# First feed-forward of a two-block transformer kernel: gate and up products as 2x2 blocks in seven instead of eight

## The chip, the cores and the metric

The kernel runs on one NeuronCore of a Trainium2 chip. The metric is the device time of one launch in microseconds (us), the median of several runs. Five engines work in parallel, and each carries out its own instructions strictly in order: TensorE (PE in the rows; PEld is its weight load), VectorE (DVE), ScalarE (ACT), GpSimd (POOL) and SyncE (SP), which here issues the DMA transfers.

## The reference, cut to what matters

Two blocks follow each other on x (512 tokens, width 1024). The first has two layers with a context of 256 tokens beside x; the second has feed-forwards, attention, a recurrence and a convolution. What is changed is the feed-forward of the first layer, which runs over x and context together, 768 tokens:

```
def swiglu(h, wg, wu, wd):
    return (jax.nn.silu(h @ wg) * (h @ wu)) @ wd
...
x = x + g_f * swiglu(rmsnorm(x) * (1 + sc_f) + sh_f, w_gate[l], w_up[l], w_down[l])
if ctx_out:
    ctx = ctx + mc[5] * swiglu(rmsnorm(ctx) * (1 + mc[4]) + mc[3], w_gate[l], w_up[l], w_down[l])
```

wg and wu are 1024 x 2816, wd is 2816 x 1024. The modulation vectors of layer 1 (`mod = silu_c @ w_ada[l] + b_ada[l]`, for x and for the context) don't depend on x, and the kernel computes most of them while this feed-forward runs.

## The kernel before, in words

All activations are kept transposed: features on the 128 partitions, the 768 tokens as columns (256 of the context, then 512 of x). A matmul in full fp32 precision is made of three matmuls in a rounded format: each operand is split into a rounded high part and the low rest (h and lo of a weight, ah and al of an activation), and `mm3` issues h*ah (L245), h*al (L246) and lo*ah (L247) for each of 8 blocks of 128 inner features. A weight tile comes by one DMA (`wtile`, L229), ScalarE copies it into the high part (L230), VectorE subtracts for the low part (L232). Activations are split likewise (`split`, L212 on ScalarE, L213 on VectorE).

`Ffn` computes a feed-forward. The 2816 inner rows are 22 blocks f of 128. For each f the weights of gate and up are loaded (512 KB each), both products are made over the 768 columns in two segments (256 and 512), `glu` takes silu of the gate on ScalarE (L409), multiplies with the up product on VectorE (L410) and splits the result. The inner rows come in groups, for the first feed-forward `G3 = ((0, 8), (8, 15), (15, 22))`; after each group the down product of its rows is made for 8 output blocks n, and VectorE adds it to x (`evac`, L1138). The last `tn` output blocks are done segment by segment so that the next phase can begin.

Ahead of the first feed-forward (phase `f0`) stands the first mixing phase, whose last part (`outproj`, then the norm with its modulation, L531 and L535) makes the activations of the feed-forward chunk by chunk; the first gate and up products are woven into it (`mm3k`, L260 to L262). Layer 1's modulation columns are made by `mod_cols`: one DMA of 512 KB (L493) a column, then for x and for the context each a product with a sum over 1024 elements, either in one VectorE instruction (L498) or as a product on GpSimd (L500) and a summing pass on ScalarE (L501). `MODV` says which. `_weave` mixes this stream with the feed-forward by declared costs (`MCOST`).

Memory is handed out by two allocators, `arena` (fp32) and `rarena` (rounded operands). A further piece, `room`, belongs to one of them at a time; `share` closes it and reopens it for the other, and everything that used it must have ended by then. The order in which each engine runs its instructions is set at build time by a scheduler that simulates a timeline; on the chip each engine then runs its list in order.

## Time and profile before

| | |
|---|---|
| median of 3 runs | 3878.45 us (3872.4 to 3878.79) |
| the profiled execution: its time, its span | 3877.54 us, 3875.8 us |
| TensorE busy | 3704.2 us, 96% of the span, mean granted clock 0.976 |
| VectorE busy | 1975.8 us, 51% |
| ScalarE busy | 1345.3 us, 35% |
| GpSimd busy | 591.6 us, 15% |
| first feed-forward, steady part | about 613 to 1100 us of the span |

The time is that of the whole launch; the span runs from the first to the last instruction. Busy shares are means over all stages, so for a change in one stage the rows of that stage are read. Times of instructions include their fill: matmuls overlap, and the distance from one start to the next is what a matmul costs.

### The profile page before, as it was taken

The page shows a single profiled execution, that of the slowest core. Times are in us where ns is not written, and L with a number is a line of the kernel's source. Part 1 is how long each engine was busy: PE and PEld are TensorE (multiplying, and loading weights), DVE is VectorE, ACT ScalarE, POOL GpSimd, SP SyncE. Part 2 cuts the span into 40 slices and gives each one's busy share as a digit, 9 for nine tenths or more (in the row PEclk, how much of TensorE's full clock was granted, in tenths as well). Part 3 has the DMA queues.
Part 4 walks back from the last instruction along what each step waited for, and adds up shares of the span by engine and source line. Part 5 has one row for each costly group of instructions (what it writes and reads, how often), then busy time and mean ns, then how long its engine had stood idle before and what let it go on. Part 6 is the DMA issues. An engine that isn't in the chain of part 4 may idle for free. (4 is left out here: it accounts for less than half of the span.)

```text
span 3875.8 us, 50567 instructions
## 1 busy us (share of the span) xinstructions
PE 3704.2 (96%) x20474; PEld 3203.6 (83%) x20474; DVE 1975.8 (51%) x3638; ACT 1345.3 (35%) x2263; POOL 591.6 (15%) x539
## 2 busy tenths in 40 slices
PE   6998899999999988999999998999999999999998
PEld 5776788888887778888988896798888888888887
DVE  8687756443254666333542358653236333736233
ACT  4233544431232354322332335443223222324222
POOL 3331012540013421000100021020002000211001
PEclk8998999999998999999999999999999999999999
DMA  5222115452202112322122321123222222312222
GB/s 208 66 93 67 39 40 181 144 181 92 61 33 74 39 65 71 103 94 91 66 95 92 110 75 51 55 90 102 81 98 98 98 75 95 109 66 98 98 94 75
DMA packets 95834, 345.12 MB, mean 89 GB/s; under 512 B 10864, under 2 KB 14064, under 8 KB 95600
## 3 DMA queue, kind: packets, MB, share of 16 engines
q1 hardware_dynamic: 95024, 341.37, 26.6%
q8 instruction: 160, 2.62, 0.3%
q14 instruction: 74, 0.61, 0.0%
q10 hardware_dynamic: 576, 0.52, 0.0%
HBM read 334.51 MB, written 4.19 MB: 87 GB/s over the span
## 5 line engine op out<-in xcount | busy, mean ns | idle before, releaser
L245 PE MATMUL psum<-rarena,room 128*128 128x512 f32 (+1 forms) x3121 | 1092.9, 351 | 5.1 <-ACT rarena L212 2.6
L247 PE MATMUL psum<-rarena,room 128*128 128x512 f32 (+1 forms) x3053 | 1076.4, 353 | 0.8 <-DVE room L232 0.8
L246 PE MATMUL psum<-rarena,room 128*128 128x512 f32 (+1 forms) x3065 | 1074.9, 351 | 0.5 <-DVE rarena L213 0.5
L247 PE MATMUL psum<-rarena 128*128 128x512 f32 (+1 forms) x2108 | 744.7, 354 | 9.9 <-DVE rarena L232 9.5
L245 PE MATMUL psum<-rarena 128*128 128x512 f32 (+1 forms) x2040 | 735.1, 361 | 16.2 <-ACT rarena L212 5.8
L246 PE MATMUL psum<-rarena 128*128 128x512 f32 (+1 forms) x2008 | 720.0, 359 | 1.3 <-DVE rarena L213 1.3
L245 PEld LDWEIGHTS psum<-rarena,room 128*128 128x128 f32 x3121 | 592.8, 190 | 82.5 <-ACT rarena L212 3.0
L246 PEld LDWEIGHTS psum<-rarena,room 128*128 128x128 f32 x3065 | 582.4, 190 | 76.0 <-DVE rarena L213 0.8
L247 PEld LDWEIGHTS psum<-rarena,room 128*128 128x128 f32 x3053 | 580.0, 190 | 78.7 <-DVE room L232 1.0
L232 DVE TENSOR_TENSOR room<-arena,room 128x1024 fp32r<-128x1024 f32 (+2 forms) x250 | 325.3, 1306 | 531.9 <-PE psum L246 231.5
L230 ACT ACTIVATE room<-arena 128x1024 fp32r<-128x1024 f32 (+2 forms) x290 | 320.1, 1110 | 738.0 <-DMA arena<-gu 242.1
L299 POOL TENSOR_TENSOR arena<-arena 128x256 f32<-128x256 f32 x170 | 136.5, 810 | 2282.8 <-ACT arena L297 2212.9
L247 PEld LDWEIGHTS psum<-rarena 128*128 128x128 f32 x2108 | 403.1, 191 | 64.2 <-DVE rarena L232 10.4
L245 PEld LDWEIGHTS psum<-rarena 128*128 128x128 f32 x2040 | 391.6, 192 | 75.5 <-ACT rarena L230 6.9
L246 PEld LDWEIGHTS psum<-rarena 128*128 128x128 f32 x2008 | 385.7, 192 | 54.6 <-DVE rarena L213 1.7
L230 ACT ACTIVATE rarena<-arena 128x1024 fp32r<-128x1024 f32 (+2 forms) x138 | 154.7, 1122 | 334.3 <-DMA arena<-gu 123.6
L232 DVE TENSOR_TENSOR rarena<-arena,rarena 128x1024 fp32r<-128x1024 f32 (+2 forms) x98 | 131.4, 1342 | 235.5 <-ACT rarena L230 114.9
L212 ACT ACTIVATE rarena<-arena 128x512 fp32r<-128x512 f32 (+2 forms) x257 | 131.2, 528 | 206.2 <-DVE arena L410 179.5
L213 DVE TENSOR_TENSOR rarena<-arena,rarena 128x512 fp32r<-128x512 f32 (+1 forms) x246 | 149.3, 622 | 87.9 <-ACT rarena L212 87.6
L297 ACT ACTIVATE arena<-arena 128x256 f32<-128x256 f32 (+1 forms) x274 | 106.9, 412 | 239.2 <-DVE arena L1230 117.3
L410 DVE TENSOR_TENSOR arena<-arena,psum 128x512 f32<-128x512 f32 (+1 forms) x170 | 100.5, 598 | 157.2 <-PE psum L247 150.9
L500 POOL TENSOR_TENSOR arena<-arena 128x1024 f32<-128x1024 f32 x48 | 125.4, 2619 | 199.9 <-DMA arena<-w_ada 88.9
(391 smaller groups left out, 4327.8 us busy)
## 6 DMA issues: line engine op xcount, KB each, us to landing
arena<-gu SPq DMA_DIRECT2D x264, 512.0 KB, 3.7
arena<-dn SPq DMA_DIRECT2D x80, 704.0 KB, 4.1
arena<-w_ada SPq DMA_DIRECT2D x60, 512.0 KB, 3.4
room<-w_ada SPq DMA_DIRECT2D x36, 512.0 KB, 4.0
room<-w_in SPq DMA_DIRECT2D x30, 512.0 KB, 3.3
arena<-c_in SPq DMA_DIRECT2D x24, 512.0 KB, 3.2
arena<-dn SPq DMA_DIRECT2D x16, 448.0 KB, 3.4
room<-ab_in SPq DMA_DIRECT2D x14, 512.0 KB, 3.2
```

What stands on the lines that cost most here:

```text
L212: A.activation(h, src, AF.Copy)
L213: eng.tensor_tensor(lo, src, h.bitcast(F32), ALU.subtract)
L230: A.activation(h.r, r.f, AF.Copy)
L232: (G if wlo[1] < wlo[0] else V).tensor_tensor(lo.r, r.f, h.f, ALU.subtract)
L245: PE.matmul(ps, h[:, s], ah, start=k == 0, stop=False)
L246: PE.matmul(ps, h[:, s], al_, start=False, stop=False)
L247: PE.matmul(ps, lo[:, s], ah, start=False, stop=k == nk - 1)
L297: A.activation(sq.f, src, AF.Square)
L299: (V if self.fast else G).tensor_tensor(self.parts[0].f, self.parts[0].f, sq.f, ALU.add)
L410: V.tensor_tensor(s.f, s.f, pu, ALU.mult)
L500: G.tensor_tensor(t.f, r.f, sic[q].f, ALU.mult)
```

## The change

The first feed-forward treats its inner blocks f = 2 to 21 as ten pairs. A pair of inner blocks (two block rows of output), the two halves of the 1024 features and the two halves of the 768 columns (384 each) form a 2x2 by 2x2 block product, which is computed with seven block products instead of eight (the form with 15 sums).

- `quads` loads the two weight tiles of gate (or up) of a pair raw, makes 4 sums of 128 x 512 and 7 splits (a copy on ScalarE, a subtract on VectorE) of 128 x 512; before, there were two splits of 128 x 1024.
- `seven_ops` and `combos` make the sums of the activation blocks once: 16 adds on GpSimd (`whole`, L555), 12 subtracts on VectorE (L562), 4 more (L390) and 12 splits, all 128 x 384. They run after the activations are complete. `third` puts the last sum in the place of one activation block once f = 1, the last plain one, is done (L580, L581).
- `Seven` makes each block product with matmuls of 384 columns (`prod`, L266 to L268) and adds the products up: per pair and per gate or up one ScalarE copy and five VectorE adds of 384 columns that read PSUM. `pair` takes silu, product and split on the four 384-column results (L603 and what follows).
- The groups of inner rows become six, `G3 = ((0, 4), (4, 8), (8, 12), (12, 16), (16, 18), (18, 22))`, so the evacuation of the down product runs six times rather than three, and its weight tiles are 128 x 512 (one group 128 x 256) rather than 1024 and 896.
- `room` is split into two parts; during the first feed-forward the first stays with `rarena` and the second goes to `arena`. The allocators' limits for temporaries are changed for that time (`BODY`), and freed extension space counts as last used when it is opened.
- All modulation products of layer 1 go to VectorE (`MODV`), so GpSimd loses 48 products and ScalarE 48 summing passes in this phase; the declared costs change (`MCOST`), and the first modulation columns are finished one by one (`each`). The number of output blocks done segment by segment at the end goes from 3 to 5 (`TN0`).

All else is the same code, but the whole program is scheduled anew.

```diff
-G3 = ((0, 8), (8, 15), (15, 22))
+G3 = ((0, 4), (4, 8), (8, 12), (12, 16), (16, 18), (18, 22))
...
-MLEN = 152 * UNIT
+ROOMS = (96 * UNIT, 56 * UNIT)
...
+        def prod(ps, w, acts, start, stop):
+
+            h, lo = w[0].r, w[1].r
+            for k, (ah, al_) in enumerate(acts):
+                s = slice(k * 128, k * 128 + 128)
+                f, e = start and k == 0, stop and k == len(acts) - 1
+                PE.matmul(ps, h[:, s], ah, start=f, stop=False, skip_group_check=True)
+                PE.matmul(ps, h[:, s], al_, start=False, stop=False, skip_group_check=True)
+                PE.matmul(ps, lo[:, s], ah, start=False, stop=e, skip_group_check=True)
...
+        def quads(src1, src2, n, eng):
+
+
+            r1, r2 = al(2 * n), al(2 * n)
+            SP.dma_start(r1.f, src1)
+            SP.dma_start(r2.f, src2)
+            a1, b1, a2, b2 = r1.f[:, :n], r1.f[:, n:], r2.f[:, :n], r2.f[:, n:]
+            yield split_new(a1, n, eng[0])
+            s2 = al(n)
+            eng[7].tensor_tensor(a1, a1, a2, ALU.subtract)
+            eng[8].tensor_tensor(s2.f, b2, a1, ALU.subtract)
+            yield split_new(s2.f, n, eng[1])
+            yield split_new(b1, n, eng[2])
+            eng[9].tensor_tensor(a2, a2, b2, ALU.add)
+            yield split_new(a2, n, eng[3])
+            yield split_new(a1, n, eng[4])
+            eng[10].tensor_tensor(s2.f, b1, s2.f, ALU.subtract)
+            yield split_new(s2.f, n, eng[5])
+            fr(s2, r1)
+            w = split_new(b2, n, eng[6])
+            fr(r2)
+            yield w
+
+        class Seven:
...
+                p = self.b[b].f
+                prod(p, w, ops[i], first, True)
+                n = self.n
+                if i == 0:
+                    self.s1 = al(n)
+                    A.activation(self.s1.f, p, AF.Copy)
+                elif i == 1:
+                    self.u2 = al(n)
+                    V.tensor_tensor(self.u2.f, p, self.s1.f, ALU.add)
+                elif i == 2:
+                    return 0, 0, p, self.b[b]
...
+                else:
+                    V.tensor_tensor(self.u2.f, p, self.u2.f, ALU.add)
+                    pf_(self.b[b])
+                    return 1, 0, self.u2.f, self.u2
...
+        def combos(src, n):
...
+                one(v[0].f)
+                two(v[1].f, v[0].f)
+                split(t2[k][0].r, t2[k][1].r, v[1].f)
+                split(t1[k][0].r, t1[k][1].r, v[0].f)
+                t = al(n, True)
+                V.tensor_tensor(t.f, v[1].f, a11, ALU.subtract)
+                t3.append(t)
+                four(v[2].f, v[1].f)
+                split(t4[k][0].r, t4[k][1].r, v[2].f)
...
+                def whole(o, i, j):
+                    u, v = self.act[k + 4 * i]
+                    sl = slice(j * h, j * h + h)
+                    G.tensor_tensor(o, u.f[:, sl], v.f[:, sl], ALU.add)
...
+                def less(i, j):
+                    def do(o, x):
+                        whole(o, i, j)
+                        V.tensor_tensor(o, o, x, ALU.subtract)
+                    return do
...
+            def third(self):
+
+                for t, (u, v) in zip(self.t3, self.ops[4]):
+                    A.activation(u, t.f, AF.Copy)
+                    V.tensor_tensor(v, t.f, u.bitcast(F32), ALU.subtract)
+                    fr(t)
+
+            def pair(self, f, hl):
...
+                    if got[0]:
+                        (r, c, g, gb), (_, _, u, ub) = got
+                        sl = slice(c * h, c * h + h)
+                        t = al(h)
...
+                            A.activation(t.f, g, AF.Silu)
+                        V.tensor_tensor(t.f, t.f, u, ALU.mult)
+                        fr(gb, ub)
+                        split(hl[r][0].r[:, sl], hl[r][1].r[:, sl], t.f)
+                        fr(t)
...
+                if seven:
+                    share(rarena, arena)
+                    temps = arena.temp, rarena.temp
+                    arena.temp, rarena.temp = BODY
+                    self.seven_ops()
...
-MODV = ((0, 1, 2, 3), (2,))
+MODV = ((0, 1, 2, 3), (0, 1, 2, 3))
...
-MCOST = 4.0
+MCOST = (3.6, 6.0)
+
+BANK = (0, 1, 0, 1, 2, 1, 2)
+BODY = (370, 530)
+SEVG = ((), ())
...
+TN0 = 5
```

Where instructions stand now, at three places.

**VectorE at the start of the first feed-forward.** The first fence has VectorE's order of before, from near the end of the splits of the last activation chunk (L213 128x256); L232 of 128x1024 is the low part of a weight tile, L498 a modulation product, L410 the gating product.

```order
L213 TENSOR_TENSOR rarena<-arena,rarena 128x256 x2
L213 TENSOR_TENSOR room<-arena,room 128x256
L213 TENSOR_TENSOR rarena<-arena,rarena 128x256 x3
L213 TENSOR_TENSOR room<-arena,rarena 128x256
L213 TENSOR_TENSOR rarena<-arena,rarena 128x256
L232 TENSOR_TENSOR room<-arena,room 128x1024
L498 SCALAR_TENSOR_TENSOR arena,mod_65<-arena 128x1024 x3
L410 TENSOR_TENSOR arena<-arena,psum 128x256
L498 SCALAR_TENSOR_TENSOR arena,mod_65<-arena 128x1024
L232 TENSOR_TENSOR rarena<-arena,rarena 128x1024
L410 TENSOR_TENSOR arena<-arena,psum 128x256
L213 TENSOR_TENSOR room<-arena,room 128x256
```

In the change the same splits (now L224 128x256) are followed by the sums of activation blocks (L562, L390) and their splits (L224 128x384); the two rows L243 of 128x1024, whose raw tiles lie in roomb, are the low parts of the weights of f = 1, L519 is the gating product and L698 the modulation product. Nine of the twelve L562 stand ahead of the first L243, four of them in this piece.

```order
L562 TENSOR_TENSOR arena<-arena 128x384 x2
L224 TENSOR_TENSOR rooma<-arena,rooma 128x384
L562 TENSOR_TENSOR arena<-arena 128x384
L224 TENSOR_TENSOR rarena<-arena,rarena 128x384
L519 TENSOR_TENSOR arena<-arena,psum 128x256
L390 TENSOR_TENSOR arena<-arena 128x384
L224 TENSOR_TENSOR rooma<-arena,rooma 128x384
L562 TENSOR_TENSOR arena<-arena 128x384
L390 TENSOR_TENSOR arena<-arena 128x384
L224 TENSOR_TENSOR rarena<-arena,rarena 128x384
L224 TENSOR_TENSOR rooma<-arena,rooma 128x256
L243 TENSOR_TENSOR rarena<-roomb,rarena 128x1024
```

The low parts of the weights of f = 1 thus moved from beside or right behind the last chunk's splits to behind most of the sums of the activation blocks.

**VectorE at the passage to the block f = 2.** In the order of before the weights of the blocks after f = 1 (L232) stand ahead of f = 1's last gating product (L410 128x512) or right behind it.

```order
L498 SCALAR_TENSOR_TENSOR arena,mod_65<-arena 128x1024
L213 TENSOR_TENSOR rarena<-arena,rarena 128x256
L498 SCALAR_TENSOR_TENSOR arena,mod_65<-arena 128x1024
L232 TENSOR_TENSOR rarena<-arena,rarena 128x1024
L232 TENSOR_TENSOR room<-arena,room 128x1024
L410 TENSOR_TENSOR arena<-arena,psum 128x512
L232 TENSOR_TENSOR room<-arena,room 128x1024
L213 TENSOR_TENSOR rarena<-arena,rarena 128x512
L498 SCALAR_TENSOR_TENSOR arena,mod_65<-arena 128x1024 x3
L232 TENSOR_TENSOR room<-arena,room 128x1024
L498 SCALAR_TENSOR_TENSOR arena,mod_65<-arena 128x1024 x2
L410 TENSOR_TENSOR arena<-arena,psum 128x256
```

In the change L519 128x512 is the last gating product of f = 1, L581 the splits of `third`, L224 of 128x512 a split (of the gated result, or of a weight quarter of the first pair), L284 a weight sum of `quads`, L715 the end of a modulation column.

```order
L581 TENSOR_TENSOR rarena<-arena,rarena 128x384 x2
L715 TENSOR_TENSOR mod_65<-mod_65,COL 128x1
L581 TENSOR_TENSOR rarena<-arena,rarena 128x384 x2
L519 TENSOR_TENSOR arena<-arena,psum 128x512
L224 TENSOR_TENSOR rarena<-arena,rarena 128x512
L698 SCALAR_TENSOR_TENSOR arena,mod_65<-roomb,arena 128x1024
L224 TENSOR_TENSOR rarena<-arena,rarena 128x512
L698 SCALAR_TENSOR_TENSOR roomb,mod_65<-roomb,arena 128x1024
L715 TENSOR_TENSOR mod_65<-mod_65,COL 128x1
L284 TENSOR_TENSOR arena<-arena 128x512
L715 TENSOR_TENSOR mod_65<-mod_65,COL 128x1
L224 TENSOR_TENSOR rarena<-arena,rarena 128x512
```

The first splits of weight quarters of the first pair now stand behind the gating product that needs f = 1's last matmul.

**GpSimd between the first mixing phase and the next.** In the order of before the 48 modulation products stand here (L299 and L408 are the squares of the norms).

```order
L213 TENSOR_TENSOR rarena<-arena,rarena 128x768 x3
L299 TENSOR_TENSOR arena<-arena 128x256 x15
L500 TENSOR_TENSOR arena<-arena 128x1024 x48
L299 TENSOR_TENSOR arena<-arena 128x256 x14
L213 TENSOR_TENSOR rarena<-arena,rarena 128x256
```

In the change it has the sums L555 of the activation blocks instead, and nothing more until the norms of the next phase (L408).

```order
L408 TENSOR_TENSOR arena<-arena 128x256 x15
L555 TENSOR_TENSOR arena<-rarena 128x384 x12
L555 TENSOR_TENSOR roomb<-rarena 128x384 x3
L555 TENSOR_TENSOR arena<-rarena 128x384
L408 TENSOR_TENSOR arena<-arena 128x256 x11
```

The 48 products have moved to VectorE, as L698.


## Rows read from the trace of the kernel before

**Rows 1.** The page's busy times, and TensorE's slices in tenths

```profile
PE 3704.2 (96%) x20474; PEld 3203.6 (83%) x20474; DVE 1975.8 (51%) x3638; ACT 1345.3 (35%) x2263; POOL 591.6 (15%) x539
...
PE   6998899999999988999999998999999999999998
```

**Rows 2.** Windows: us, busy us and instructions by engine, granted clock, DMA share, GB/s

```profile
505.00:613.00 108.00, 103.36 (x723) 96.08 (x721) 62.74 (x152) 42.30 (x87) 12.88 (x16) 1.00 0.22 73
613.00:1100.00 487.00, 486.94 (x2803) 431.28 (x2804) 203.94 (x250) 157.40 (x250) 129.38 (x54) 1.00 0.38 124
1100.00:1180.00 80.00, 71.62 (x516) 68.44 (x515) 54.72 (x161) 34.39 (x83) 24.91 (x29) 0.89 0.13 47
```

**Rows 3.** TensorE's timeline, two segments of 21 and 24 matmuls: start, duration, instruction

```profile
525.70 0.40 PE L245 MATMUL psum<-rarena,room 128*128 128x512 f32 x1
...
530.49 0.28 PE L245 MATMUL psum<-rarena,room 128*128 128x256 f32 x1
...
533.36 0.40 PE L245 MATMUL psum<-rarena,room 128*128 128x512 f32 x1
```

**Rows 4.** TensorE's timeline elsewhere: matmuls of 384 columns

```profile
2399.00 0.44 PE L1485 MATMUL psum<-rarena 128*128 128x384 f32 x1
2399.28 0.34 PE L1486 MATMUL psum<-rarena 128*128 128x384 f32 x1
2399.46 0.28 PE L1485 MATMUL psum<-rarena 128*128 128x256 f32 x1
```

**Rows 5.** VectorE by line and shape, 613 to 1100: busy, mean ns, idle and releasers

```profile
L232 DVE TENSOR_TENSOR room<-arena,room 128x1024 fp32r<-128x1024 f32 x28 | 39.5, 1412 | 44.4 <-ACT room L230 24.3 <-PE psum L246 17.1 <-issue 2.9
L498 DVE SCALAR_TENSOR_TENSOR arena<-arena 128x1024 f32<-128x1024 f32 x26 | 31.6, 1224 | 32.7 <-DMA arena<-w_ada 32.5
L213 DVE TENSOR_TENSOR rarena<-arena,rarena 128x512 fp32r<-128x512 f32 x21 | 23.9, 1140 | 12.3 <-ACT rarena L212 12.3
...
L1138 DVE SCALAR_TENSOR_TENSOR arena<-psum,mod,arena 128x512 f32<-128x512 f32 x20 | 14.9, 747 | 26.4 <-PE psum L247 26.4
...
L1138 DVE SCALAR_TENSOR_TENSOR arena<-psum,mod,arena 128x256 f32<-128x256 f32 x20 | 9.6, 482 | 21.0 <-PE psum L247 21.0
```

**Rows 6.** VectorE's timeline at the start of the first feed-forward

```profile
591.72 0.41 DVE L213 TENSOR_TENSOR rarena<-arena,rarena 128x256 fp32r<-128x256 f32 x1
...
612.93 0.68 DVE L410 TENSOR_TENSOR arena<-arena,psum 128x512 f32<-128x512 f32 x1
613.53 1.22 DVE L232 TENSOR_TENSOR room<-arena,room 128x1024 fp32r<-128x1024 f32 x1
...
616.52 1.22 DVE L498 SCALAR_TENSOR_TENSOR arena<-arena 128x1024 f32<-128x1024 f32 x1
...
617.67 1.22 DVE L498 SCALAR_TENSOR_TENSOR arena<-arena 128x1024 f32<-128x1024 f32 x1
```

**Rows 7.** GpSimd by line and shape, the same stretch, then its adds of 384 elsewhere

```profile
L500 POOL TENSOR_TENSOR arena<-arena 128x1024 f32<-128x1024 f32 x48 | 125.4, 2619 | 199.9 <-DMA arena<-w_ada 88.9 <-ACT arena L409 57.8 <-DVE room L232 33.9
...
L880 POOL TENSOR_TENSOR arena<-arena 128x384 f32<-128x384 f32 x14 | 14.9, 1085 | 11.1 <-PE psum L863 11.1
```

**Rows 8.** VectorE's, then GpSimd's timeline, 651 to 657

```profile
651.14 0.68 DVE L410 TENSOR_TENSOR arena<-arena,psum 128x512 f32<-128x512 f32 x1
652.51 1.73 DVE L213 TENSOR_TENSOR rarena<-arena,rarena 128x512 fp32r<-128x512 f32 x1 [0.70 <-ACT rarena L212]
...
651.29 5.20 POOL L500 TENSOR_TENSOR arena<-arena 128x1024 f32<-128x1024 f32 x2 [5.13 <-DVE room L232]
```

**Rows 9.** TensorE's timeline, the wait ahead of the block f = 2

```profile
611.02 0.28 PE L245 MATMUL psum<-rarena 128*128 128x256 f32 x1
613.06 0.39 PE L245 MATMUL psum<-rarena,room 128*128 128x256 f32 x1 [1.76 <-ACT room L230]
```

**Rows 10.** DMA issues, 560 to 1100: KB each, median us from issue to landing

```profile
arena<-gu SPq DMA_DIRECT2D x42, 512.0 KB, 3.9
```

**Rows 11.** Windows of 20 us, columns as in rows 2

```profile
2300.00:2320.00 20.00, 17.52 (x127) 16.82 (x128) 15.88 (x38) 8.36 (x19) 9.44 (x12) 0.91 0.26 88
```

More of the change, by code (lines that the diff above doesn't have):

```diff
@@ L64, with __init__ @@
 class _Arena:
[L67 to L71 removed]
+    def __init__(self, ap, n, unit, temp=0, rounded=False, more=()):
+        self.unit, self.temp, self.rounded = unit, temp // unit, rounded
+        self.parts, o = [], 0
+        for m in (n, *more):
+            self.parts.append([o, m // unit, None])
+            o += m // unit + 1
+        self.freed = np.full(o, np.inf)
         self.clock = 0
+        self.extend(0, ap)
     def al(self, n, long=False):
@@ L77, in al @@
         f = self.freed
-        top = (len(f) if self.parts[1] is not None else self.n0) - self.temp
+        top = max(o + m for o, m, ap in self.parts if ap is not None) - self.temp
         for lo in (0,) if long or not self.temp else (top, 0):
@@ L287, in bcast_r @@
             fr(rb)
+        def combos(src, n):
+            t1, t2, t4 = ([alhl(n) for _ in range(KD // 2)] for _ in range(3))
+            t3 = []
+            for k in range(KD // 2):
+                a11, one, two, four, free = src(k)
+                v = [al(n) for _ in range(3)]
+                one(v[0].f)
[7 more added lines that the diff above has]
+                split(t4[k][0].r, t4[k][1].r, v[2].f)
+                fr(v)
+                free()
+            return t1, t2, t3, t4
         class Rms:
@@ L1232, in evac @@
                         post.square(n, sl)
-            return Ffn(f"ffn2_{l}{i}", S, G2, gu[f], dn[f], first.begin if first else None, prepf, evac, post.finish, HF, TN, late)
+            return Ffn(f"ffn2_{l}{i}", S, G2, gu[f], dn[f], first.begin if first else None, prepf, evac, post.finish, HF, TN, late, NF,
+                       [[G if i in SEVG[0] else V for i in range(11)]] * 2)
         class Mix2(Phase):
```

167 lines of the change are left out of this document (123 added, 44 removed).

## The prediction

> **What bounds the kernel now.** I read the page's busy times first: TensorE is busy 96% of the span, no other engine over 51% [rows 1]. Then the windows around the first feed-forward [rows 2]: from 613 to 1100 us TensorE is busy 486.94 of 487.00 us at full clock, while VectorE is busy 203.94, ScalarE 157.40 and GpSimd 129.38. So this stage is bound by TensorE alone, and each microsecond of matmul taken out of it counts, as long as the others keep up. Ahead of it (505 to 613) TensorE idles 4.6 us of 108, behind it (1100 to 1180) 8.4 of 80: there the chains through the other engines set the time. I forecast against the profiled execution, 3877.54 us; the median of the three runs is 0.9 us more, which changes nothing. A difference of 0.2%, 7.8 us, is about what a measurement of this kernel tells from none.
>
> **1. Matmuls removed.** What a matmul costs is the distance between starts. 21 of 512 columns take 530.49 − 525.70 = 4.79 us, 0.228 each; 24 of 256 columns take 533.36 − 530.49 = 2.87 us, 0.1196 each [rows 3]. Twenty inner blocks, gate and up, 8 feature blocks and 3 matmuls make 960 of each size: 960 x 0.3477 = 333.8 us. The change makes 10 pairs x 2 x 7 products x 4 blocks x 3 = 1680 matmuls of 384 columns. This stage has none, so the mean of the two sizes, 0.1738, is my estimate: 292.0 us. One row elsewhere has 0.18 from start to start, another 0.28 behind a narrower kind [rows 4]; at 0.1987 the whole gain would be gone. The two sizes here lie on a line with a small fixed part, so I take 0.174, with 0.18 (a saving of 31 us) as the other end. Term: **−41.7 us** (−31 to −42). A pair goes from 33.4 to 29.2 us.
>
> **2. VectorE's new load.** Start to start a VectorE instruction of 512 elements costs 613.53 − 612.93 = 0.60 us, one of 1024 elements 617.67 − 616.52 = 1.15 us [rows 6], so one of 384 about 0.46. Per pair: 14 splits and 8 weight sums of 512 (13.2 us), 10 additions, 4 gating products and 4 splits of 384 (18 x 0.46 = 8.3 us), together 21.5. The modulation products number 26 on VectorE and 48 on GpSimd in this stretch now [rows 5, 7]; all 74 on VectorE are 85 us, five a pair (5.75). That gives 27.2 us a pair against 29.2 of matmuls: just under. Over the stage: 216 for pairs, 85 for modulation, 6 x 8 evacuations of each segment at 0.75 and 0.48 [rows 5] 59 us, 48 smaller weight tiles of the down product 27, the activation sums and their splits 15: about 400 us in some 470. VectorE stays below TensorE on the mean, but at 85% of it instead of 42%; hardly any slack is left for a stall to be caught up. ScalarE loses 48 summing passes and has room.
>
> What speaks for the load being bearable: GpSimd's products vanish. While they run, VectorE's splits with both operands in memory stretch: 1.73 us for a split of 512 at 652.51, beside GpSimd's products from 651.29 on, where a gating product that reads PSUM took 0.68 [rows 8], and the mean of such splits in the stage is 1.14 us [rows 5]. That delay goes away; it is hidden under TensorE today, so it earns nothing by itself.
>
> [...]
>
> **3. The start of the stage.** Before, the last split of the last activation chunk ends at 592.1 [rows 6], f = 1's weights are ready about then, and the block f = 2 starts at 613.06, behind a wait of 1.76 us [rows 9]. In the new order VectorE must do, between that split and the second low part of f = 1's weights, 11 sums and 9 splits of 384 (9.2 us), a gating product and a split of 256 (0.7) and the two weights (2.3): 12.2 us, so 604.3 at the earliest. The sums also wait for GpSimd: 16 adds of 384 at 1.0 to 1.1 us (2619 ns scaled from 1024 columns to 384, and a row of that size at 1085 ns [rows 7]). Half of them need the last chunk; if VectorE's two-operand sums and splits can't run beside them, as in rows 8, these 8 us come on top: 612. Moreover f = 1's raw tiles now lie in the second part of the room, which is reopened only once its last reader has ended; then come 3.9 us of DMA [rows 10] and a copy. That ends in the same window. f = 1 itself is 48 x 0.3477 = 16.7 us of matmuls, so it ends between 621 and 629. Then the first pair waits: its first weight splits stand behind f = 1's last gating product, so 0.68 + 0.60 + 1.15 + 0.68 = 3.1 us and some hand-overs. The first pair starts at 624 to 632, 11 to 19 us later than f = 2 now. A pause of TensorE also costs clock: a slice with 2.5 us idle ran at 0.91 of full clock, 1.8 us lost in 20 [rows 11]. Term: 12 to 21, I take the middle, **+16 us**. [...]
>
> **4. Later joints.** Each of the 9 other pairs can wait at its start for such a chain of 3 to 4 us (34 us in all), if VectorE runs behind; nothing, if it runs ahead. The raw tiles of a pair are freed only late in it, and five passages between down products and pairs are new or earlier in the order. VectorE's slack is 2 us a pair, which mostly covers it. I take a quarter: **+8 us** (3 to 14).
>
> **5. The rest.** The two-part room and the new costs reorder all other stages; TN0 = 5 puts two more output blocks segment by segment at the passage, where VectorE is already busy 54.72 of 80 us [rows 2]. No row prices it; the idle around the passage is 4.6 and 8.4 us, and I let it move by a good half of that: **+2 us** (−4 to +6).
>
> Sum: −41.7 + 16 + 8 + 2 = −15.7, so 3877.54 − 15.7 = **3862 us**.
>
> **Rivals.**
>
> *The joints cost little.* GpSimd's adds lie beside work that doesn't collide, the pairs run ahead: start +11, joints +3, rest −2: −29.7, 3848 us. For it: VectorE's mean of 85%. Against: rows 8.
>
> *VectorE becomes the bound.* If the instructions follow one another by their full durations, 22 x 0.68 + 18 x 0.55 + 5 x 1.22 = 31.0 us a pair, 1.8 more than the matmuls, 18 us over ten pairs; part of the joints is in that (4 of 8). 3862 + 18 − 4 = 3876 us. For it: 85% leaves little, and there are waits between engines in each product's addition. Against: starts 0.60 apart in a busy stretch.
>
> *Every pair waits for its raw tiles* (slower). If the tiles of the next pair can be fetched only when this one's are freed, then a DMA of 3.9 us [rows 10], a copy and a low part (0.6 + 0.7) stand bare at each of nine joints: 5.2 x 9 = 47 instead of 8, 3862 + 39 = 3901 us. It decides from 3.5 us a joint on. For it: 512 KB tiles, four a pair, in a memory that is nearly full. Against: the second part of the room goes to the raw tiles.
>
> *A matmul of 384 columns costs more than the mean of its neighbours.* At 0.20 the matmuls take 336 us and nothing is saved: 3877.54 + 2 + 26 = 3906 us. Against: rows 3's line.
>
> **Chances.** My forecast (3853 to 3871) 0.45; joints cost little 0.20; VectorE the bound (3871 to 3880) 0.20; waits for raw tiles 0.08; dearer matmuls 0.04; still faster, below 3844, 0.03. Faster by over 0.2% (below 3870.7): forecast, cheap joints and the last, 0.68. Slower (above 3886): raw tiles, dearer matmuls and a tail of the VectorE case, 0.13. Within: 0.19. The range that leaves out no more than 2 in 10 reaches from the cheap joints to the VectorE case: 3845 to 3881.
>
> **What would show it.** In the profile after: 384-column matmuls 0.174 apart and gate and up of a pair in 29 us; TensorE's busy time down by about 42; VectorE's splits of 512 back to 0.68; a gap of TensorE of 11 to 19 us, in one or two pieces, between the last activation chunk and the first pair, ended by VectorE's low parts (L243) or by the DMA behind the room; and gaps of a few us at the starts of some pairs. The forecast is wrong if matmuls of 384 are 0.19 or more apart, if VectorE is busy without a break through the pairs while TensorE waits, or if the wait for raw tiles returns in each pair.

## The result, and the profile after

The change is slower: 3910.26 us (median of 4 runs, 3909.86 to 3916.64) against 3875.97 us before, a ratio of 1.0087, 95% interval 1.0074 to 1.0099. The forecast was 3862 us, range 3845 to 3881. The profiled execution's span is 3908.5 us, 32.7 more than before.

The page's busy times of the changed kernel, then TensorE's slices:

```profile
PE 3690.3 (94%) x20231; PEld 3218.5 (82%) x20231; DVE 2183.7 (56%) x4134; ACT 1357.5 (35%) x2327; POOL 484.8 (12%) x507
...
PE   6998897999989989999999998999999999999998
```

TensorE works 14 us less than in [rows 1] and the span is 33 longer. The windows of [rows 2] show where (columns as there):

```profile
505.00:613.00 108.00, 94.39 (x658) 88.10 (x656) 66.85 (x146) 38.57 (x87) 31.63 (x31) 0.96 0.11 33
613.00:1100.00 487.00, 463.75 (x2596) 435.19 (x2597) 390.41 (x712) 160.56 (x294) 4.28 (x2) 0.98 0.36 120
1100.00:1180.00 80.00, 68.99 (x468) 65.57 (x466) 58.21 (x179) 34.87 (x80) 16.78 (x21) 0.91 0.30 99
```

Where TensorE was busy all of 487.00 us it now idles 23, VectorE went from 204 to 390 us, and already ahead of 613 TensorE is busy 9.0 us less. To see the stages I set four marks by TensorE's starts: W, the last woven product at the stage's start (L262 before, L350 after); P, the first matmul of the first pair (before: of f = 2); N, the first one-column matmul of the first norm of the passage (L311, L420); E, the last woven product of the passage. The rest of the program is read at the last woven product of all. For P before, [rows 9] is not the place: its wait at 613.06 lies inside f = 2. f = 1's last matmul starts at 608.28, and f = 2's first product comes right behind it, in TensorE's timeline of before:

```profile
608.51 0.28 PE L245 MATMUL psum<-rarena 128*128 128x256 f32 x1
```

| us | before | after | lost since the mark before |
|---|---|---|---|
| W | 597.1 | 605.4 | 8.3 |
| P | 608.5 | 643.8 | 27.1 |
| N | 1112.9 | 1140.5 | −7.8 |
| E | 1164.7 | 1194.3 | 2.0 |
| last woven product of all | 3529.6 | 3562.4 | 3.2 |

From W to P, 16.7 of the change's 38.5 us are f = 1's matmuls and 18.4 two waits, shown below. Before, 5.4 us of f = 1's matmuls had been done ahead of W, between the woven products, and the others followed without a break.

From P to N the change's matmuls alone would take 292.0 (pairs) + 106.7 + 71.3 (468 matmuls of 512 and 596 of 256 columns, nearly all of the down products) = 470.0 us. It took 496.6, so 26.6 us were lost there; before it was 1.5 (502.9 of 504.4). In 16.0 of the 26.6 TensorE stood idle; some 7 of the rest are matmuls that came slower in the 6 us behind a wait. The 20 us behind P, which follow a wait of 5.22 us, have hardly any idle time, but the mean granted clock is 0.87: from 645.05 to 648.57 the matmuls of 384 columns start 0.32 us apart, from 649.46 on 0.174:

```profile
643.80:663.80 20.00, 19.96 (x101) 19.74 (x102) 15.26 (x28) 7.96 (x15) 0.00 (x0) 0.87 0.01 1
```

Behind N lay 126 matmuls of 256 columns of the down product before and 52 after, 15.1 and 6.2 us, inside the passage, whose length hardly changed (51.8 and 53.8); 8.9 of the saving had only filled its gaps.

TensorE's timeline, products of 384 columns in the steady part (start, duration, instruction):

```profile
699.77 0.33 PE L266 MATMUL psum<-rarena 128*128 128x384 f32 x1
699.95 0.33 PE L267 MATMUL psum<-rarena 128*128 128x384 f32 x1
...
700.64 0.33 PE L268 MATMUL psum<-rarena 128*128 128x384 f32 x1
700.82 0.28 PE L258 MATMUL psum<-rooma,rarena 128*128 128x256 f32 x1
```

Six matmuls in 1.05 us, 0.175 each: that price was right. The timeline at the two waits ahead of the first pair:

```profile
618.77 0.58 PE L256 MATMUL psum<-rarena 128*128 128x256 f32 x1 [13.13 <-ACT rarena L241]
...
643.84 0.69 PE L266 MATMUL psum<-rarena 128*128 128x384 f32 x1 [5.22 <-ACT rarena L223]
```

VectorE's timeline, the sums of the activation blocks, with GpSimd's adds:

```profile
605.21 1.36 DVE L224 TENSOR_TENSOR rooma<-arena,rooma 128x384 fp32r<-128x384 f32 x1
606.49 1.34 DVE L562 TENSOR_TENSOR arena<-arena 128x384 f32<-128x384 f32 x1
607.76 1.35 DVE L224 TENSOR_TENSOR rooma<-arena,rooma 128x384 fp32r<-128x384 f32 x1
...
614.57 0.55 DVE L562 TENSOR_TENSOR arena<-arena 128x384 f32<-128x384 f32 x1
```

```profile
597.55 12.41 POOL L555 TENSOR_TENSOR arena<-rarena 128x384 f32<-128x384 f32 x9 [6.98 <-DVE rarena L224]
```

GpSimd's nine adds take 12.41 us in all, and three more follow until 613.8. From 604 on, while they run, VectorE's instructions of 384 start 1.27 us apart; when GpSimd is done, 0.47. ScalarE copies in order behind those sums, and SP issues late:

```profile
617.67 1.04 ACT L241 ACTIVATE rarena<-roomb 128x1024 fp32r<-128x1024 f32 x1
...
643.16 0.63 ACT L223 ACTIVATE rarena<-arena 128x512 fp32r<-128x512 f32 x1 [3.15 <-DMA arena<-gu]
```

```profile
605.19 1.30 SPq L240 DMA_DIRECT2D roomb<-gu  x2
...
637.28 0.33 SPq L280 DMA_DIRECT2D arena<-gu  x1
637.75 0.33 SPq L279 DMA_DIRECT2D arena<-gu  x1
```

f = 1's raw tiles are issued at 605.19, when the last reader of the room's second part has ended, and by [rows 10] would have been there by about 610, but the copy L241 stands in ScalarE's queue until 617.67. The first pair's raw tiles are issued at 637 to 638 and ScalarE's first split of them waits for them until 643.16. What SP's queue waited for from 600 to 1130 (total us, times, longest):

```profile
SPq L693 <- DVE rarena L224: 135.4, 23, 20.6
...
SPq L280 <- DVE rarena L581: 7.0, 1, 7.0
```

Its transfers wait for instructions that free memory; the first pair's waited for `third` (L581), which frees the last activation sums.

The two longest waits between P and N, in TensorE's, ScalarE's, VectorE's and SP's timelines, and what SP's queue waited for from 1060 to 1079:

```profile
1082.87 0.69 PE L266 MATMUL psum<-rarena 128*128 128x384 f32 x1 [3.33 <-ACT rarena L223]
...
1082.19 1.15 ACT L223 ACTIVATE rarena<-roomb 128x512 fp32r<-128x512 f32 x2 [4.62 <-DMA roomb<-gu]
...
1082.85 1.29 DVE L224 TENSOR_TENSOR rarena<-roomb,rarena 128x512 fp32r<-128x512 f32 x2 [2.71 <-ACT rarena L223]
...
1078.19 0.33 SPq L279 DMA_DIRECT2D roomb<-gu  x1
...
SPq L279 <- DVE rarena L224: 1.4, 1, 1.4
...
1118.10 0.39 PE L256 MATMUL psum<-rarena,rooma 128*128 128x256 f32 x1 [2.73 <-DVE arena L1341]
...
1116.41 1.23 DVE L698 SCALAR_TENSOR_TENSOR arena<-arena 128x1024 f32<-128x1024 f32 x1 [2.29 <-DMA arena<-w_ada]
```

The first is a raw tile: its transfer waited for a split that frees memory, landed 4.0 us after its issue, and VectorE was idle too. In the second, VectorE's evacuation (L1341) stands in order behind a modulation product that waited for its column.

### The profile page after: what moved, and what is told of

Its sections match the earlier page's. It is cut to its first block, busy times and chain, and to the rows that moved or that the text cites. A ratio compares the mean times of both kernels' runs of the same rounds, so it can differ in the third digit from the quotient of the medians.

```text
span 3908.5 us, 50807 instructions
## 1 busy us (share of the span) xinstructions
PE 3690.3 (94%) x20231; PEld 3218.5 (82%) x20231; DVE 2183.7 (56%) x4134; ACT 1357.5 (35%) x2327; POOL 484.8 (12%) x507
## 5 line engine op out<-in xcount | busy, mean ns | idle before, releaser
L256 PE MATMUL psum<-rarena 128*128 128x512 f32 (+1 forms) x1996 | 715.4, 362 | 30.3 <-ACT rarena L241 15.5
L258 PE MATMUL psum<-rarena 128*128 128x512 f32 (+1 forms) x2060 | 732.5, 358 | 5.7 <-DVE rarena L243 5.7
L257 PE MATMUL psum<-rarena 128*128 128x512 f32 (+1 forms) x1996 | 714.0, 359 | 0.8 <-DVE rarena L224 0.8
L256 PE MATMUL psum<-rarena,rooma 128*128 128x512 f32 (+1 forms) x1667 | 595.3, 358 | 10.0 <-DVE arena L1341 4.2
L257 PE MATMUL psum<-rarena,rooma 128*128 128x512 f32 (+1 forms) x1667 | 595.0, 357 | 1.8 <-DVE rarena L224 1.7
L258 PE MATMUL psum<-rarena,rooma 128*128 128x512 f32 (+1 forms) x1676 | 595.7, 356 | 0.1
L408 POOL TENSOR_TENSOR arena<-arena 128x256 f32<-128x256 f32 x170 | 140.7, 834 | 2589.7 <-ACT arena L406 2521.0
L256 PEld LDWEIGHTS psum<-rarena 128*128 128x128 f32 x1996 | 384.1, 193 | 89.1 <-ACT rarena L241 18.2
L256 PEld LDWEIGHTS psum<-rarena,rooma 128*128 128x128 f32 x1667 | 317.1, 191 | 55.6 <-DVE arena L1341 4.8
L257 PEld LDWEIGHTS psum<-rarena,rooma 128*128 128x128 f32 x1667 | 317.4, 191 | 47.6 <-DVE rarena L224 3.2
L258 PEld LDWEIGHTS psum<-rarena,rooma 128*128 128x128 f32 x1676 | 318.0, 190 | 44.5 <-DVE rooma L243 0.2
L241 ACT ACTIVATE rooma<-arena 128x1024 fp32r<-128x1024 f32 (+2 forms) x168 | 183.0, 1094 | 420.3 <-DMA arena<-gu 146.0
L243 DVE TENSOR_TENSOR rooma<-arena,rooma 128x1024 fp32r<-128x1024 f32 (+2 forms) x132 | 167.8, 1276 | 269.5 <-PE psum L257 142.1
L257 PE MATMUL psum<-rarena,roomb 128*128 128x512 f32 (+1 forms) x833 | 292.8, 352 | 1.3 <-DVE rarena L224 1.3
L256 PE MATMUL psum<-rarena,roomb 128*128 128x512 f32 (+1 forms) x833 | 293.0, 352 | 0.0
L258 PE MATMUL psum<-rarena,roomb 128*128 128x512 f32 (+1 forms) x760 | 270.0, 356 | 0.0
L241 ACT ACTIVATE rarena<-arena 128x1024 fp32r<-128x1024 f32 (+3 forms) x144 | 151.3, 1052 | 339.8 <-DMA arena<-gu 106.9
L243 DVE TENSOR_TENSOR rarena<-arena,rarena 128x1024 fp32r<-128x1024 f32 (+3 forms) x113 | 133.3, 1182 | 219.8 <-PE psum L257 98.7
L223 ACT ACTIVATE rarena<-arena 128x512 fp32r<-128x512 f32 (+3 forms) x312 | 166.8, 551 | 251.7 <-DVE arena L519 132.6
L224 DVE TENSOR_TENSOR rarena<-arena,rarena 128x512 fp32r<-128x512 f32 (+2 forms) x303 | 179.1, 606 | 69.2 <-ACT rarena L223 66.2
```

Of the source, the lines that this page charges most:

```text
L223: A.activation(h, src, AF.Copy)
L224: eng.tensor_tensor(lo, src, h.bitcast(F32), ALU.subtract)
L241: A.activation(h.r, r.f, AF.Copy)
L243: (G if wlo[1] < wlo[0] else V).tensor_tensor(lo.r, r.f, h.f, ALU.subtract)
L256: PE.matmul(ps, h[:, s], ah, start=k == 0, stop=False)
L257: PE.matmul(ps, h[:, s], al_, start=False, stop=False)
```

## The experiments

Marks and medians of all runs (us; W to P only where there are pairs). Every run is scheduled anew from where its edit first tells, so differences of a few us between them can be order alone. The ratio is to the kernel before, timed again beside each run; its median was then between 3871.72 and 3878.85, so medians of different runs are compared by the ratio.

| run | W | W to P | P to N | W to N | N to E | median | ratio |
|---|---|---|---|---|---|---|---|
| before | 597.1 | 11.4 | 504.4 | 515.8 | 51.8 | 3875.97 | 1 |
| the change | 605.4 | 38.5 | 496.6 | 535.1 | 53.8 | 3910.26 | 1.0087 |
| e1 sums on VectorE | 607.0 | 34.3 | 493.6 | 528.0 | 54.6 | 3904.96 | 1.0084 |
| e2 f = 1's weights first | 611.3 | 28.9 | 506.1 | 535.0 | 57.2 | 3902.66 | 1.0076 |
| e3 both | 605.2 | 25.5 | 503.5 | 529.0 | 59.1 | 3899.47 | 1.0068 |
| e7 e3, first raw tiles first | 605.9 | 11.2 | 514.2 | 525.4 | 52.0 | 3886.84 | 1.0030 |
| e12 e7, three tail blocks | 613.9 | 11.2 | 517.9 | 529.1 | 51.6 | 3895.91 | 1.0034 |
| e14 e7, columns on GpSimd's queue | 605.9 | 11.2 | 515.0 | 526.2 | 55.6 | 3897.35 | 1.0053 |
| e8 no products | 607.0 | 36.3 | 489.4 | 525.7 | 53.1 | 3901.99 | 1.0069 |
| e9 no columns | 613.4 | 37.7 | 474.9 | 512.6 | 56.1 | 3901.10 | 1.0060 |
| e11 columns on GpSimd's queue | 605.0 | 38.8 | 494.2 | 533.0 | 55.2 | 3916.08 | 1.0092 |
| e4 products on GpSimd | 606.6 | 38.5 | 524.0 | 562.5 | 53.9 | 3936.56 | 1.0148 |
| e16 8 units held | 606.7 | 36.8 | 514.8 | 551.6 | 60.3 | 3924.06 | 1.0126 |
| e15 rooms of 64 and 88 | 620.2 | 32.2 | 746.2 | 778.4 | 55.5 | 4170.07 | 1.0755 |
| e18 the same, sums on VectorE | 619.8 | 27.3 | 752.6 | 780.0 | 55.9 | 4170.96 | 1.0760 |
| e5 plain | 605.2 | | | 519.7 | 55.3 | 3886.81 | 1.0038 |
| e10 plain, one room | 613.3 | | | 518.1 | 51.1 | 3877.84 | 1.0007 |
| e17 e10, old costs | 597.3 | | | 521.0 | 57.9 | 3886.11 | 1.0026 |
| e19 e7, no columns | 616.8 | 11.2 | 482.3 | 493.5 | 53.1 | 3861.35 | 0.9959 |
| e20 plain, no columns | 617.5 | | | 516.7 | 54.7 | 3883.89 | 1.0019 |

**The start of the stage.** e1 puts the whole adds on VectorE, e2 loads f = 1's weights before the room is handed over, e3 does both:

```diff
-                    G.tensor_tensor(o, u.f[:, sl], v.f[:, sl], ALU.add)
+                    V.tensor_tensor(o, u.f[:, sl], v.f[:, sl], ALU.add)
...
                 if seven:
+                    first = self.wf(self.hf)
                     share(rarena, arena)
...
-                            ws = self.wf(f)
+                            ws = first if seven and f == self.hf else self.wf(f)
```

e1: 

> The 16 whole adds of the activation blocks (L555) go from GpSimd to VectorE; nothing else. Theory A (in the trace of the change VectorE and GpSimd take turns from 597 to 614 us, 1.27 us a VectorE instruction of 384 instead of 0.47): VectorE does 16 adds of 0.47 more but loses some 13 delays of 0.8, the copies of f = 1's weights on ScalarE come earlier, TensorE's wait of 13.1 us at 618.8 shrinks to 5 to 8 (the raw tiles of f = 1 were issued only at 605.2), whole time 5 to 8 us below the change, about 3903. Rival B (the start is held by the raw tiles of the first pair, which are issued at 637): the first pair starts no earlier than 640 us, time within 3 us of the change.

e2: 

> f = 1's weight tiles are loaded before the room is handed over and before the activation sums; the sums stay on GpSimd and VectorE. Theory A: f = 1 starts right behind the woven products at about 605 us, the wait of 13.1 us goes, f = 1 lies over the sums; the first pair then waits for the sums or its raw tiles at some 630: time 10 to 16 us below the change, about 3897. Rival B: the first pair's raw tiles keep their time (issued at 637), so f = 1's earlier start is lost in front of the first pair; time within 3 us of the change.

e3: 

> Both edits. Theory A: gap ahead of f = 1 gone and no taking of turns; first pair at about 625 us instead of 643.8; time 16 to 20 us below the change, about 3892, still above before, because the losses in the pairs, at the passage and in the other stages stay. Rival B: within 3 us of the change.

e1 gained 4 us from W to P and 7 from W to N, but its ratio, 1.0084, can't be told from the change's: the turns are gone, and the first pair still starts at 641.3. e2 lost its wait ahead of f = 1 and waited 15.4 us ahead of the first pair instead; from W to N it gained nothing. So both theories held a part: the sums and f = 1's weights cost their time, but the first pair came hardly earlier (641.3 and 640.2 against 643.8). e3 gained 13 us from W to P, 6 from W to N and by its ratio some 7 in all, less than theory A's 16 to 20. In e3, TensorE's and SP's timelines:

```profile
630.65 0.69 PE L266 MATMUL psum<-rarena 128*128 128x384 f32 x1 [14.38 <-ACT rarena L223]
```

```profile
614.39 0.33 SPq L694 DMA_DIRECT2D arena<-w_ada  x1
627.01 1.47 SPq L279 DMA_DIRECT2D arena<-gu  x2
```

The raw tiles go out at 627.01, and TensorE waits 14.38 us. e7 asks for their memory ahead of the sums:

```diff
+                    self.rr = [raws(kn(self.gu_f[p, :, i]), kn(self.gu_f[p + 1, :, i]), 512) for i in range(2)]
                     self.seven_ops()
```

e7: 

> On top of both edits of the run before (sums on VectorE, f = 1's weights first): memory and transfers of the first pair's four raw weight tiles are asked for ahead of the activation sums, so that they don't wait for the memory of those sums. Theory A (in the run with both edits the first pair waited 14.4 us because its raw tiles were issued at 627, behind the last use of the sums' memory): the first pair starts at 617 to 621 instead of 630.7, the wait shrinks to under 4 us. Theory V (the pairs are then held by VectorE's queue, which has the same work to do): most of that is lost again before the first norm, time 0 to 5 us under the run with both edits (3899). Rival: the gain stays, time 8 to 12 us under it.

The first pair starts 11.2 us behind W, as f = 2 before (11.4): the whole loss at the start is gone, 27 us. But only 9.7 of them are left at N. TensorE's timeline of e7:

```profile
626.47 0.69 PE L266 MATMUL psum<-rarena,rooma 128*128 128x384 f32 x1 [5.03 <-ACT roomb L320]
...
644.67 0.69 PE L266 MATMUL psum<-rarena,rooma 128*128 128x384 f32 x1 [7.88 <-ACT rooma L223]
```

The waits moved into the first two pairs. Theory V had that right: of the 14 us that e3's first pair still lost, 3.6 are left at N. Its time missed all the same, 3886.84 being 13 us under e3, because the passage (7 us) and the later stages were shorter too. In the end e7 is 3886.84 us, ratio to before 1.0030 (1.0019 to 1.0042), still slower.

**What holds the pairs.** e8 leaves out the modulation products on VectorE, e9 their transfers as well:

```diff
+                    if not skip:
                         (G if MODQ else SP).dma_start(r.f, w_ada[l, j])
...
+                        if skip:
+                            V.memset(acc, 0.0)
-                        if j % 4 in MODV[l]:
+                        elif j % 4 in MODV[l]:
```

e8: 

> The change, with the modulation products on VectorE in this stage left out (the columns are set to 0; their transfers stay), so the output is not the reference's. VectorE loses some 85 us between 600 and 1110. Theory V (VectorE at 80% and in order is what costs the pairs their gain): the stretch from the first pair to the first norm takes 470 to 478 us instead of 496.6, time some 20 us below the change. Rival M (raw tiles wait for memory, behind the transfers of the modulation columns on SP's queue): the stretch stays above 488 us.

e9: 

> The change, with the modulation columns of this stage left out altogether, products and transfers (set to 0; the output is not the reference's). Theory V: like the run without products, 470 to 478 us for the stretch and no more than 4 us better than it. Rival M: 470 to 478 here, but not in the run that keeps the transfers.

VectorE freed of 78 us of work (396 to 318 from P to N) shortens the stretch by 7.2 us, so theory V's 470 to 478 missed; without the columns it is 21.7 shorter, as rival M said (9.4 and 22.5 from W to N). So VectorE's load makes up about a third of the 21.7, and 14.5 us hang on the columns' transfers or memory. DMA issues between 600 and 1100 in the change, then in e9 (KB each, median us to landing):

```profile
arena<-gu SPq DMA_DIRECT2D x29, 512.0 KB, 4.0
...
roomb<-gu SPq DMA_DIRECT2D x13, 512.0 KB, 4.5
```

```profile
arena<-gu SPq DMA_DIRECT2D x29, 512.0 KB, 3.4
roomb<-gu SPq DMA_DIRECT2D x13, 512.0 KB, 4.0
```

Without the columns' traffic a raw tile lands 0.5 to 0.6 us sooner; at ten pairs that is some 6 us, if it stood bare once a pair. The rest is memory, or the place in the queue. e11 and e14 move the transfers to GpSimd's queue:

```diff
-                    (G if MODQ else SP).dma_start(r.f, w_ada[l, j])
+                    (G if l or each else SP).dma_start(r.f, w_ada[l, j])
```

e11: 

> The change, with the transfers of this stage's modulation columns issued from GpSimd's queue, which is idle there, instead of SP's. Theory Q (raw weight tiles stand on SP's queue behind column transfers that wait for memory, 135 us of waits of that kind on SP's queue in the change): the stretch from the first pair to the first norm falls from 496.6 to 480 to 486 us, time 8 to 15 us below the change. Theory S (space itself is short, whatever the queue): the stretch stays within 5 us of 496.6; the gain of the run without columns then came from the memory that they hold.

e14: 

> The run with the first raw tiles ahead of the sums (3886.84), with the column transfers of this stage on GpSimd's queue. Theory Q: its stretch from the first pair to the first norm, 514.2 us with waits of 5.0 and 7.9 us in the first two pairs, falls to 490 or less, time 10 to 20 us below it, about 3872, level with before. Theory S: over 505 us, time within 6 us of it.

Stretches of 494.2 and 515.0 us: the queue is not it, theory Q falls. e16 holds 8 of the 276 units of fp32 memory, unused, and nothing else:

```diff
+                    held = al(8 * UNIT)
                     self.seven_ops()
```

e16: 

> The change, with 8 units of 64 floats of the fp32 memory (of 276) held unused through the stage. Theory S (space: raw tiles and modulation columns of 16 units each wait for one another's memory): the stretch from the first pair to the first norm grows from 496.6 to 503 us or more, time 5 to 20 us above the change. Theory V (VectorE's queue alone costs the pairs their gain): the stretch stays within 4 us of 496.6.

The stretch grew by 18.2 us and the median by 14. TensorE's timeline of e16, three of the waits that the change doesn't have:

```profile
680.17 0.58 PE L256 MATMUL psum<-rooma,rarena 128*128 128x256 f32 x1 [4.99 <-ACT rarena L241]
...
886.74 0.58 PE L256 MATMUL psum<-rarena 128*128 128x256 f32 x1 [4.54 <-ACT rarena L241]
...
956.76 0.69 PE L266 MATMUL psum<-rarena,rooma 128*128 128x384 f32 x1 [6.11 <-ACT rooma L223]
```

The last of them, in SP's and ScalarE's timelines, with what SP's queue waited for from 940 to 951:

```profile
SPq L280 <- ACT roomb L603: 5.8, 1, 5.8
...
950.13 0.33 SPq L279 DMA_DIRECT2D roomb<-gu  x1
...
956.08 0.63 ACT L223 ACTIVATE rooma<-roomb 128x512 fp32r<-128x512 f32 x1 [4.90 <-DMA roomb<-gu]
```

The transfers of the raw tiles waited for an instruction that frees memory and landed bare. That is what memory at its limit looks like: 3% less of it costs two thirds as much again as all the losses of the stretch. The opposite was tried by moving 32 units of the room to the fp32 side:

```diff
-ROOMS = (96 * UNIT, 56 * UNIT)
+ROOMS = (64 * UNIT, 88 * UNIT)
```

e15: 

> The change, with the two parts of the room at 64 and 88 units instead of 96 and 56: 32 units, two raw tiles, more of fp32 memory in the stage, 32 fewer for the rounded operands. Theory S: the stretch falls from 496.6 to 478 to 490 us, unless the rounded operands, now short themselves, take it back. Theory V: within 4 us of 496.6. The first mixing phase is ordered anew, so the whole time says little; the stretch decides.

e18: 

> The same rooms of 64 and 88 units, with the whole adds on VectorE. Theory S: stretch 478 to 490 us, first pair 2 to 6 us earlier behind the woven products than in the change; time 8 to 20 us below the change (3910). Theory V: stretch within 4 us of the 493.6 that the run with the adds on VectorE had.

Both missed: 746 and 753 us. The rounded operands, 32 units shorter, starve, and the waits are for splits into the room in every pair. So these two say nothing about a gain by fp32 memory alone; they say that the rounded side is at its limit too. e4 puts three quarters of layer 1's products back on GpSimd:

```diff
-MODV = ((0, 1, 2, 3), (0, 1, 2, 3))
+MODV = ((0, 1, 2, 3), (2,))
```

e4: 

> The change, with three quarters of layer 1's modulation products back on GpSimd (and their sums on ScalarE). VectorE loses some 55 us in the stage, but its splits and weight sums with two operands in memory meet GpSimd's products of 2.4 us. Theory K (the meeting costs more than the relief: all products left out gave back only 7 us in the stretch): stretch 505 to 540 us, time 10 to 40 us above the change. Rival V: relief wins, stretch 488 to 494.

Theory K holds: the stretch is 27 us longer. VectorE by line and shape, 645 to 1140, in e4, and 645 to 1110 in the change (busy, mean ns):

```profile
L243 DVE TENSOR_TENSOR rarena<-arena,rarena 128x512 fp32r<-128x512 f32 x16 | 23.6, 1478 | 4.7 <-ACT rarena L241 4.6
```

```profile
L224 DVE TENSOR_TENSOR rarena<-arena,rarena 128x512 fp32r<-128x512 f32 x68 | 46.1, 685 | 8.6 <-ACT rarena L223 6.3 <-PE psum L267 2.3
...
L243 DVE TENSOR_TENSOR rarena<-arena,rarena 128x512 fp32r<-128x512 f32 x16 | 10.9, 685 | 5.1 <-ACT rarena L241 4.8 <-PE psum L267 0.3
```

The down product's low parts take 1478 ns beside GpSimd's products and 685 without. Without this part the change would have been slower still.

**What the seven are worth, and the rest.** e5 has the change without the seven (`NF` in place of `NF if l else 2`); e10 also one room; e17 also `MCOST = (4.0, 4.0)`.

e5: 

> The products in seven are switched off in the first feed-forward (all 22 inner blocks plain); six groups, two-part room (the second part stays with the rounded operands), modulation on VectorE, the declared costs and the five tail blocks stay. Theory C (half of the loss has nothing to do with the seven: 8.6 us already in the first mixing phase, 12 at the passage, some 7 in later stages, all from the new schedule): slower than before by 15 to 27 us, about 3895 to 3902. Rival D (all losses come with the products in seven and their sums): within 6 us of before, 3870 to 3882.

e10: 

> The run without the products in seven, and the room in one part again. Theory R (the 8 us lost in the first mixing phase come from the room in two parts): the woven products at the start of the feed-forward end at 597 instead of 605, time 5 to 10 us below the plain run (3887), about 3879. Rival: the new declared costs or other edits reorder that phase; it ends at 603 to 607 as before, time within 3 us of the plain run.

e17: 

> No products in seven, the room in one part and the old declared costs: of the change there remain the six groups, the modulation on VectorE, the five tail blocks. The first mixing phase has the order of before, so its woven products end at 597. Theory C (the loss in the first mixing phase is the new order of that phase and nothing on the chip): they end at 596 to 599. The whole time 3866 to 3880; if six groups or the tail cost time by themselves, above 3884.

e5 is slower than before by 0.38% (0.22 to 0.55), 15 us, the lower end of theory C, without any product in seven. Its TensorE doesn't wait in the steady part:

```profile
800.00:900.00 100.00, 99.95 (x576) 88.11 (x575) 50.18 (x82) 22.04 (x34) 0.00 (x0) 1.00 0.43 145
```

VectorE's order up to W is almost the same in e5 and in the change, and so is W (605.2, 605.4). In e10 theory R missed: W is at 613.3, not 597, and the median came right for another reason, since the second mixing phase, ordered otherwise, ended 0.9 us before that of the kernel before. In e17 VectorE's order up to W is that of before but for a few places, and W is at 597.3: the 8 us ahead of the stage come from the first mixing phase's new order, and not from the parts of the change that e17 keeps. But e17 gives them back behind W: 5 us more than before from W to N and 6 at the passage, median 3886.11. That missed its 3866 to 3880 and lies above its mark of 3884 for six groups or the tail costing time by themselves; which of them does, or whether it is order again, stays open. e12 has `TN0 = 3` on top of e7:

e12: 

> The run with the first raw tiles ahead of the sums (3886.84), with three output blocks done segment by segment at the passage, as before the change, instead of five. Theory T (the longer tail costs the passage: from the first norm to the end of the woven products 53.6 us in the change with 7 us of the down product left, 51.5 before with 17 left): time 5 to 12 us below that run. Rival (the passage is a chain of norms whose length doesn't hang on the tail): within 5 us of it.

N to E is 51.6 against 52.0 us: theory T falls, and the rival's chain of fixed length holds. The rival's 5 us for the whole time were missed (W came 8 us later in e12), though the ratios, 1.0030 and 1.0034, are the same within their intervals. Over all runs the passage takes 51 to 60 us, whatever is left of the down product.

Last, the seven with the columns' memory free: e19 is e7, e20 is e5, both without the columns.

e19: 

> The run with the first raw tiles ahead of the sums, with this stage's modulation columns left out (transfers, memory and products; the columns are 0, the output is not the reference's). Theory S (the products in seven lose to the want of memory, not by themselves): first pair within 16 us behind the woven products, stretch from the first pair to the first norm 470 to 480 us, the stage from the woven products' end at its start to the one at the passage 545 to 560 us, against 588.9 in the change.

e20: 

> Its counterpart: no products in seven, this stage's modulation columns left out as well (output not the reference's). The stage was 575.0 us in the plain run, where TensorE was busy without a break; without columns 568 to 575. Theory S: the run with the products in seven and no columns is 15 to 35 us faster than this one. Rival V: within 10 us, since the seven's own sums and chains eat the gain even with memory free.

W to E is 546.6 us in e19 and 571.4 in e20, 24.8 less with the seven; medians 3861.35 and 3883.89, 22.5 apart. P to N missed its bounds by 2 us (482.3), since the first pair, started early, still waits 4.6 us in itself. The windows of e19, then of e20:

```profile
800.00:900.00 100.00, 100.00 (x577) 96.00 (x576) 65.26 (x112) 34.23 (x61) 0.00 (x0) 1.00 0.21 71
```

```profile
800.00:900.00 100.00, 100.00 (x577) 88.45 (x576) 32.78 (x48) 22.57 (x34) 0.00 (x0) 1.00 0.21 69
```

TensorE is full in both, with VectorE at 65 us of 100 in the first. So theory S holds and rival V falls: the seven's own sums and chains let more than half of the 41.7 us through once the columns are gone. These two take away the columns' products, transfers and memory together. That the columns' memory takes more of it in the change than VectorE's 78 us rests on e8, e9, e11 and e16 together; how the 14.5 us divide between memory and traffic was not measured apart. Apart from e19, which leaves the columns out, no version was faster than the kernel before; the nearest, e10, has no products in seven.

## Why the prediction was wrong, by its steps

- **Step 1, matmuls removed: right.** −41.7 us; spacing 0.174 to 0.175.
- **Step 2, VectorE's load: right as a mean, and not the bound.** 396 us busy from P to N were forecast as some 400 over the stage. Instructions of 512 start 0.60 apart (702.54 to 703.14 in the change). Freed of 78 us, the stretch gains 7.
- **Step 3, the start: right mechanisms, 27.1 us in place of 16, outside its 12 to 21.** VectorE and GpSimd took turns, and the room was reopened late. Two links were missing: ScalarE's copy of f = 1's weights stood in order behind the copies of the sums, and the first pair waited for raw tiles whose memory the activation sums held, not for VectorE. e7 shows both by taking the whole term away. The step also took the wait of [rows 9] for the start of f = 2, which is at 608.51, so its base was 4.6 us late: counted from the true start, its 624 to 632 are a loss of 15 to 23 us.
- **Step 4, the later joints: the step whose mechanism failed.** "VectorE's slack is 2 us a pair, which mostly covers it. I take a quarter: +8 us." It was 25.1 more than before (26.6 against 1.5). The step asked whether an engine had time; what the pairs lack, by e8, e9, e11 and e16 together, is memory more than VectorE's time. A pair's four raw tiles of 16 units live through six or seven of its products, beside modulation columns of 16 units each, in 276. My slower rival had this place, raw tiles that wait for freed memory, at 47 us and a chance of 0.08; against it I set that the room's second part goes to the raw tiles. e16 shows how full it is all the same. The wait did not return in every pair, as that rival had it; the waits lie at some starts of pairs and around the down products.
- **Step 5, the rest: +2 in place of some 22, the term that was furthest off.** 8.3 by the order of the first mixing phase (e17), 10.9 at the passage (8.9 of down products that had filled its gaps, and 2.0), 3 later. I let the passage move by its idle time, and did not see that doing less ahead of a chain of fixed length is no gain where the work had filled that chain. What of the later stages' shifts belongs to which edit stays open: e5, e10 and e17 move them by up to 19 us without any product in seven.

The sum of what was measured: −41.7 + 27.1 + 25.1 + 8.3 + 10.9 + 3.2 = 32.9 us, but for rounding the difference of the spans, 32.7. The rival of VectorE as the bound is refuted by e8, that of dearer matmuls by the spacing. None of the three signs that the prediction set for being wrong showed: the loss came in several places at once, and steps 3, 4 and 5 were each too low, by 11, 17 and 20 us.

## What to carry to other kernels

Fewer products with more operands were paid here in memory more than in engine time: count what each raw operand holds and how long, beside all that is prefetched in the same stage, and hold a little memory back as a test of how near the limit is. Before crediting a saving on the engine that bounds a stage, look at what the saved work was covering behind it. When the whole program is ordered anew, run the change with its main part switched off; here all but the main part cost 15 us.

## What the runs showed of the hardware

From 604 to 614 us in the change VectorE's sums and splits of 384 columns, with two operands in SBUF, and GpSimd's adds of 384 take turns one for one: the starts lie 1.27 us apart on both engines, against 0.47 on VectorE behind the last add (614.10 to 614.57), so each VectorE instruction comes 0.80 us later beside an add. Six us earlier the turns were not one for one; GpSimd's, then VectorE's timeline:

```profile
597.55 2.78 POOL L555 TENSOR_TENSOR arena<-rarena 128x384 f32<-128x384 f32 x1 [6.98 <-DVE rarena L224]
597.71 1.76 DVE L224 TENSOR_TENSOR rarena<-arena,rarena 128x256 fp32r<-128x256 f32 x5
```

Five VectorE splits of 256 columns went through 0.33 us apart, as with no add running (596.07 to 596.40), and the one add, 1.00 us elsewhere (600.29), took 2.78: 1.78 more, about the 1.76 that the five splits took.
